# Dense attention scores: the products with the keys' low parts as two tiles of 64 rows, on a copied query

## The chip, the cores and the metric

The kernel runs on one core of a Trainium2 chip. The metric is the device time of one execution in microseconds (us). The kernel before was timed in three runs: 2363.53, 2365.14 and 2366.84 us, a median of 2365.14. One further execution was taken with the hardware profiler; every duration below is from it. Engines in the rows: PE is the tensor engine (PEld its loading of weights), DVE the vector engine, ACT the scalar engine, POOL the GpSimd engine, SP the engine that issues most transfers; an ending q (ACTq, SPq) is an engine's issuing of transfers.

## The reference

A trunk of two layers over 1024 tokens of width 1024. Each layer has three groups of attention heads beside each other (A: four heads with a two-dimensional neighbourhood, B: six with a sliding window, C: six dense heads on two key and value heads), an output projection and a gated feed-forward part. The change is in group C:

```python
q = apply_axial_rope(rms_norm(q, gq), cos, sin)      # (1, 1024, 6 heads, 64)
k = apply_axial_rope(rms_norm(k, gk), cos, sin)      # (1, 1024, 2 groups, 64)
# for each block of 128 queries, R = 3 heads per group
s = jnp.einsum('bqgrd,bkgd->bgrqk', qblk, k).astype(jnp.float32) * scale
p = jax.nn.softmax(s, axis=-1).astype(v.dtype)
return jnp.einsum('bgrqk,bkgd->bqgrd', p, v)
```

So a head has 8 blocks of 128 queries, and each block needs scores against all 1024 keys, a softmax over them, and the product with the values. The computation is in float32.

## The kernel before, in words

**High and low parts.** PE takes the type fp32r here, which holds fewer bits than float32. To keep precision the kernel splits numbers into a high part, rounded to fp32r, and a low part, the remainder. For group C, the tile `qkC[g]` (128 rows, 5 slots, 1024 tokens; one per key group) holds in slots 0 to 2 the three query heads, transposed: rows 0 to 63 are the 64 dimensions of the high part, rows 64 to 127 those of the low part. Slot 3 holds the keys' high part twice, one below the other, and slot 4 the keys' low part twice. One product over all 128 rows with slot 3 so gives (query high + query low) x key high, and one with slot 4 gives (query high + query low) x key low.

**A block of scores.** `c_dots` (line 1356) takes head and block, and makes a tile `sC` of 128 queries by 1024 keys in PSUM: for each half of 512 keys a product with slot 3 and then one with slot 4, which adds to it. These are four products of 128x512 with the same 128x128 weights, the query block. DVE takes the row maximum (`c_max`, a TENSOR_REDUCE into `rs`), ACT the exponential with the row sum (`c_exp`, an ACTIVATE into `pr`), and POOL divides by the sum (`scale_rows`). Then PE transposes the block in eight pieces of 128x128 (tiles `T`, four pieces each), ACT casts each tile of four to its high part (`pt`), DVE subtracts for the low part (also `pt`), and PE multiplies with the values (`pv<-pt,vs`). PSUM has two buffers for `sC`, three for `T` and one for `pv`.

**The order.** Two blocks of a head make a pair (class `PairC`, line 1586); 24 pairs of C come first in a stream, then 16 of A and 24 of B. A loop over n (line 1879) handles pair n: it turns (transposes) pair n, multiplies pair n-1 with the values, and scores the pair three ahead (`AHEAD`). Pairs 0 and 1 are scored earlier, during the projections; pairs 2 and 3 in `opened`, at n = 0. In this stage, from n = 0 to 22, PE, ACT and DVE aren't pinned to the written order: a scheduler orders their instructions ahead of time, by its own estimates. POOL keeps the written order, and so does SP up to n = 6.

**Transfers in that stage.** At n = 0 eight transfers on SP store the values to DRAM (`v_store`, rows `vAd<-vs`); at n = 6 eight bring them back in another layout, for groups A and B (`v_back`, rows `vs<-vAd`). In layer 0, at n = 4, SP also stores a skewed bias table for A and rows for B (`skA<-skr`, `skB<-rowB`). Behind these stand the loads for the first A heads (`qk<-qkd`, `zA<-zAd`). All of SP's and ACT's transfers share eight semaphores (DMAHW0 to DMAHW7), given out in turn; a transfer waits until the transfer before it on the same semaphore has landed. Which of them this is shows from the built program.

The recording helper at line 49 issues every operation, so rows of the profile nearly all have line 49; they are told apart by the tiles' names.

Of the kernel before, what the change touches and what calls it, by code (L numbers as in the profile page):

```python
# [11 lines left out]
F32R = mybir.dt.float32r  # L12
# [7 lines left out]
P = 128  # L20
# [56 lines left out]
def f32(ap):  # L77
    return ap.bitcast(F32)
# [7 lines left out]
def trunk(ctx: ExitStack, tc, A, C, out):  # L86
    nc = tc.nc
    pe, act, dve, pool, sp = (
        Engine(tc, e) for e in (nc.tensor, nc.scalar, nc.vector, nc.gpsimd, nc.sync)
    )  # L90

    def pin(engines, on):
        for e in engines:
            e.pinned = on

    def open_pool(name, bufs=1, side="left", space=None):
        kw = dict(name=name, bufs=bufs, side=side, reuse_waits="tile")
        if space is not None:
            kw["space"] = space
            if space == PSUM:  # L100
                kw.pop("side")
        cm = tc.tile_pool(**kw)
        p = cm.__enter__()
        return cm, p
# [156 lines left out]
    class Ahead:  # L261


        def __init__(self, gen):
            self.gen, self.have = gen, []
# [141 lines left out]
    def rstd_cols(ssqs, width, nt, sp_, psp, tag="mm", newton=False):  # L407

        ps = psp.tile([P, 512], F32, name="ps_st", tag=tag)
        for j in range(nt):  # L410
            for i, s in enumerate(ssqs):
                pe.matmul(
                    ps[:, j : j + 1],
                    s[:, j * P : (j + 1) * P],
                    ones,
                    start=(i == 0),
                    stop=(i == len(ssqs) - 1),
                )
        r = sp_.tile([P, 8], F32, name="rstd", tag="rstd", bufs=2)
        if newton:  # L420
            inv_sqrt(r[:, :nt], ps[:, :nt], width, sp_)
            return r
        act.activation(r[:, :nt], ps[:, :nt], AF.Sqrt, bias=epst, scale=1.0 / width)
        dve.reciprocal(r[:, :nt], r[:, :nt])
        return r
# [592 lines left out]
    for l in range(2):  # L1018
# [14 lines left out]
        def qk_tile():  # L1033
            return qkp.tile([P, 5, S], F32R, name="qk", tag="qk", bufs=2)

        qkC = [qk_tile() for _ in range(2)]
# [313 lines left out]
        def c_scores(h, j, c, pr, rs):  # L1350

            s = c_dots(h, j)
            c_max(s, c, rs)
            c_exp(s, c, pr, rs)

        def c_dots(h, j):

            g = qkC[h // 3]
            s = psS.tile([P, 1024], F32, name="sC", tag="S")
            for kb in range(2):  # L1360
                ks = slice(kb * 512, (kb + 1) * 512)
                for i in range(2):
                    pe.matmul(
                        s[:, ks], g[:, h % 3, j * P : (j + 1) * P], g[:, 3 + i, ks],
                        start=(i == 0), stop=(i == 1),
                    )
            return s

        def c_max(s, c, rs):
            dve.tensor_reduce(out=rs[:, c : c + 1], in_=s, axis=AX.X, op=ALU.max, negate=True)  # L1370
# [61 lines left out]
        for oc in range(NE, 8):  # L1432
            w = wab
            for half in range(2):
# [16 lines left out]
                i = 2 * (oc - NE) + half  # L1451
# [20 lines left out]
        at_cm, atp = open_pool("att", side="right")  # L1472
# [114 lines left out]
        class PairC(Pair):  # L1587
            def __init__(self, h, p):
                super().__init__(10 + h, 6 + h // 3, p)
                self.h = h  # L1590
                self.pr = first_pairs.pop(0) if first_pairs else [None, None]

            def dots(self, c):
                self.s = getattr(self, "s", []) + [c_dots(self.h, 2 * self.p + c)]

            def max(self, c):
                c_max(self.s[c], c, self.rs)
# [152 lines left out]
        class PairA(Band):  # L1750


            name, by_columns = "sA", True
# [11 lines left out]
        class PairB(Band):  # L1765
            name = "sB"
# [109 lines left out]
        AHEAD, AHEAD_B, NC = 3, 4, 24  # L1876
        pin((pool,), True)
        made, done = 0, len(first_pairs)
        scored, worked = [], []
        for n in range(-AHEAD - 1, N + 3):  # L1880
            ahead = AHEAD if n + AHEAD < NC else AHEAD_B
# [25 lines left out]
            else:  # L1907
# [18 lines left out]
                        pairs[n - 1].pv(i)  # L1926
                scored, worked = fresh, scored
            done = max(done, min(begin.stop, made)) if n >= 0 else done
            while made < min(N, n + ahead + 2):
                for key, make in preload.get(made, []):  # L1930
                    heads[key] = make()
                pairs[made] = stream[made][0]()
                made += 1
# [31 lines left out]
            for end, (chunks, width) in norms.items():  # L1965
                if begins[end] <= m <= end and (m - begins[end]) % 8 == 7 and (n <= NC or m >= NC):
                    i = (m - begins[end]) // 8
# [55 lines left out]
        for ki in range(5):  # L2023
# [8 lines left out]
            if ki == 2:  # L2032
                r = rstd_cols([gss[N - 1]], norms[N - 1][1], 8, atp, psl, newton=True)
# [503 lines left out]
        for u in range(NU):  # L2537
            i, t = divmod(u, NB)
# [14 lines left out]
            for j in range(4):  # L2553
                js = slice(j * P, (j + 1) * P)
# [39 lines left out]
        if last_layer:  # L2594
            blocks_ = [(1, j, nh) for j in range(4) for nh in range(2)]
            turned = [out_turn(*b) for b in blocks_[:7]]
            r = rstd_cols(odd, D, 4, ntp, psl)
# [105 lines left out]
```

## Time and profile before

| what | value |
|---|---|
| runs | 2363.53, 2365.14, 2366.84 us; median 2365.14 |
| span of the profiled execution | 2365.0 us |
| PE busy in it | 2324.0 us, 98% |
| DVE, ACT, POOL busy | 1758.8, 1185.8, 778.4 us |
| score products of C (`sC<-qk`) | 384 of 400 ns mean, 106.2 us |
| row maxima of C (`rs<-sC`) | 88 of 1220 ns, 107.4 us |

The span is within the spread of the runs, so the profiled execution can stand for them. A row of a group reads: line, engine, operation, output<-input by the names of tiles, shape, count | busy us, mean ns of one | idle time of the engine just before them, and what ended most of it. A row of the timeline reads: start, duration, engine, line, operation, tiles, count of operations run together, and in brackets the idle time before. PE's operations are pipelined: the recorded length of one is longer than the pace at which they follow each other, so the number of 384 times 400 ns is not time that PE spends on them alone (106.2 us counts overlaps once).

### The profile page before, as it was taken

Reading aid. Unit: us, or ns where it says so; the run is one execution under the profiler, and the core shown is the slowest. Engines: PE = TensorE matmul, PEld = TensorE weight load, DVE = VectorE, ACT = ScalarE, POOL = GpSimd, SP = SyncE. Lnnn points to the kernel's source line nnn. Section 1 sums busy time; section 2 is a strip of 40 time slices with the busy share of each in tenths; the row PEclk is TensorE's granted clock in tenths of the full one; section 3 lists DMA queues with packets and bytes.
Section 4 is the critical chain, followed back from the end, with each engine's and each line's share of the span. In section 5 each row is a group of like instructions: output and inputs, shape, how many; then the busy total and the mean of one; then the engine's idle time right before and its main releaser. Section 6 shows DMA issues by size and latency. Waiting matters only on the chain. (4 is left out here: it accounts for less than half of the span.)

```text
span 2365.0 us, 33492 instructions
## 1 busy us (share of the span) xinstructions
PE 2324.0 (98%) x11804; PEld 1959.2 (83%) x11804; DVE 1758.8 (74%) x2762; ACT 1185.8 (50%) x2262; POOL 778.4 (33%) x749
## 2 busy tenths in 40 slices
PE   9999999999999999999999999999999999999998
PEld 7888898888788888788888889988878888888886
DVE  7878998869867677595767689897796674538765
ACT  5423889845543333344633268896453434334443
POOL 1530447600444445100145134584005444430001
PEclk9999999999999999999999999999999999999999
DMA  8677416162435544775435851333634443339643
GB/s 281 182 213 232 116 34 185 51 210 94 146 121 166 165 138 141 232 233 181 148 102 139 249 177 28 92 104 104 208 98 139 151 147 103 99 107 305 203 120 112
DMA packets 307450, 358.02 MB, mean 151 GB/s; under 512 B 52029, under 2 KB 223901, under 8 KB 307281
## 3 DMA queue, kind: packets, MB, share of 16 engines
q1 hardware_dynamic: 290784, 346.26, 47.1%
q10 hardware_dynamic: 16128, 9.44, 1.5%
q8 instruction: 93, 1.52, 0.3%
q14 instruction: 77, 0.62, 0.1%
q0 software_dynamic: 368, 0.17, 0.0%
HBM read 270.84 MB, written 88.63 MB: 152 GB/s over the span
## 5 line engine op out<-in xcount | busy, mean ns | idle before, releaser
L49 PE MATMUL ps_d<-wpt 128*128 128x512 f32 x1848 | 423.7, 390 | 1.0 <-ACT wpt L49 0.7
L49 PEld LDWEIGHTS ps_d<-wpt 128*128 128x128 f32 x1848 | 345.7, 188 | 74.3 <-issue 3.0
L49 POOL TENSOR_SCALAR pr<-pr,rs 128x1024 f32<-128x1024 f32 (+2 forms) x248 | 190.7, 785 | 186.8 <-DVE rs L49 166.7
L49 POOL TENSOR_TENSOR sg<-sg,u 128x512 f32<-128x512 f32 x82 | 117.2, 1431 | 348.1 <-ACT sg L49 221.6
L49 ACT CAST wpt<-w 128x512 fp32r<-128x512 f32 x154 | 95.7, 621 | 194.5 <-PE ps_d L49 176.1
L49 PE MATMUL pv<-pt,vs 128*128 128x256 f32 x1088 | 174.0, 296 | 14.3 <-DVE y L49 13.0
L49 DVE TENSOR_TENSOR pt<-T,pt 128x512 fp32r<-128x512 f32 x272 | 177.4, 679 | 7.1 <-ACT pt L49 5.9
L49 ACT CAST pt<-T 128x512 fp32r<-128x512 f32 x272 | 151.7, 586 | 42.9 <-PE T L49 41.4
L49 DVE SCALAR_TENSOR_TENSOR acc<-wmt,condT,acc 128x512 f32<-128x512 f32 (+1 forms) x98 | 115.5, 1186 | 77.1 <-DMA wmt<-in_w_mod_dram 76.3
L49 POOL TENSOR_TENSOR wpt<-ws,wpt 128x512 fp32r<-128x512 f32 x80 | 112.8, 1410 | 181.6 <-ACT wpt L49 136.3
L49 ACT COPY u<-ps_w 128x512 f32<-128x512 f32 x128 | 75.1, 587 | 192.6 <-PE ps_w L49 192.6
L49 DVE TENSOR_TENSOR wpt<-w,wpt 128x512 fp32r<-128x512 f32 x154 | 109.0, 708 | 83.8 <-ACT wpt L49 83.8
L49 PEld LDWEIGHTS pv<-pt,vs 128*128 128x128 f32 x1088 | 141.0, 189 | 26.9 <-DVE y L49 24.9
L49 PE MATMUL T<-identr,pr 128*128 128x128 f32 x1176 | 160.1, 273 | 0.8 <-DVE pt L49 0.4
L49 PEld LDWEIGHTS T<-identr,pr 128*128 128x128 f32 x1176 | 137.8, 140 | 15.8 <-issue 1.3
L49 ACT CAST wpt<-ws 128x512 fp32r<-128x512 f32 x176 | 107.7, 622 | 53.3 <-PE ps_w L49 23.4
L49 DVE TENSOR_TENSOR wpt<-graw,wpt 128x512 fp32r<-128x512 f32 x154 | 110.2, 716 | 17.0 <-ACT wpt L49 17.0
L49 DVE TENSOR_TENSOR wpt<-ws,wpt 128x512 fp32r<-128x512 f32 x96 | 85.2, 896 | 47.6 <-ACT wpt L49 47.4
L49 DVE TENSOR_REDUCE rs<-sC 128x1 f32<-128x1024 f32 x88 | 107.4, 1220 | 12.3 <-PE sC L49 10.9
L49 DVE TENSOR_TENSOR ws<-wr 128x512 f32<-128x512 f32 x88 | 80.3, 913 | 48.5 <-POOL wpt L49 45.1
L49 ACT CAST wpt<-graw 128x512 fp32r<-128x512 f32 x154 | 95.0, 617 | 35.2 <-DMA graw<-gpd 31.0
L49 PE MATMUL ps_w<-h22h,wpt 128*128 128x512 f32 x352 | 108.9, 391 | 2.9 <-ACT u L49 1.9
(310 smaller groups left out, 5936.4 us busy)
## 6 DMA issues: line engine op xcount, KB each, us to landing
wr<-in_w_gu_dram SPq DMA_DIRECT2D x92, 512.0 KB, 4.2
gpd<-sg SPq DMA_DIRECT2D x154, 256.0 KB, 4.4
graw<-gpd SPq DMA_DIRECT2D x76, 512.0 KB, 3.8
w<-in_w_down_dram SPq DMA_DIRECT2D x110, 256.0 KB, 5.2
wmt<-in_w_mod_dram SPq DMA_DIRECT2D x48, 512.0 KB, 5.7
qk<-qkd SPq DMA_DIRECT2D x44, 512.0 KB, 7.3
wst<-in_w_o_dram SPq DMA_DIRECT2D x32, 512.0 KB, 4.3
wmt<-in_w_mod_dram SPq DMA_DIRECT2D x64, 256.0 KB, 4.0
```

What stands on the lines that cost most here:

```text
L49: ins = op(*args, **kwargs)
```

## The change

```diff
-        def c_dots(h, j):
-
-            g = qkC[h // 3]
+        def high_again(h, j):
+
+            q = atp.tile([P, P], F32R, name="qd", tag="qd", bufs=10)
+            act.dma_start(
+                f32(q[64:128, :]), f32(qkC[h // 3][0:64, h % 3, j * P : (j + 1) * P])
+            )
+            return q
+
+        def c_dots(h, j, qd=None):
+
+            g, js = qkC[h // 3], slice(j * P, (j + 1) * P)
             s = psS.tile([P, 1024], F32, name="sC", tag="S")
-            for kb in range(2):
-                ks = slice(kb * 512, (kb + 1) * 512)
-                for i in range(2):
-                    pe.matmul(
-                        s[:, ks], g[:, h % 3, j * P : (j + 1) * P], g[:, 3 + i, ks],
-                        start=(i == 0), stop=(i == 1),
-                    )
+            halves = [slice(kb * 512, (kb + 1) * 512) for kb in range(2)]
+            q = g[:, h % 3, js]
+            for ks in halves:
+                pe.matmul(s[:, ks], q, g[:, 3, ks], start=True, stop=False)
+            for kb, ks in enumerate(halves):
+                r = slice(kb * 64, kb * 64 + 64) if qd is not None else slice(0, P)
+                qr = qd[r] if kb and qd is not None else q[r]
+                pe.matmul(s[:, ks], qr, g[r, 4, ks], start=False, stop=True)
             return s
...
                 self.pr = first_pairs.pop(0) if first_pairs else [None, None]
+                self.qd = again.pop((h, p), [None, None])
 
             def dots(self, c):
-                self.s = getattr(self, "s", []) + [c_dots(self.h, 2 * self.p + c)]
+                self.s = getattr(self, "s", []) + [c_dots(self.h, 2 * self.p + c, self.qd[c])]
...
         made, done = 0, len(first_pairs)
+        again, qmade = {}, 6
...
             done = max(done, min(begin.stop, made)) if n >= 0 else done
+            while 0 <= n and qmade < min(NC, n + AHEAD + 4):
+                h, p = divmod(qmade, 4)
+                again[h, p] = [high_again(h, 2 * p + c) for c in range(2)]
+                qmade += 1
             while made < min(N, n + ahead + 2):
```

`c_dots` now issues both products with slot 3 first, over all 128 rows as before, and then both with slot 4. Where a block has a copy `qd`, the slot-4 product for keys 0 to 511 runs on rows 0 to 63 alone (the query's high part with the keys' low part), and the one for keys 512 to 1023 on rows 64 to 127. For that the query's high part has to stand in rows 64 to 127 as well: `high_again` copies it there from rows 0 to 63 of `qkC`, by a transfer within the chip's memory that ACT issues (64 rows of 512 bytes). The product of the query's low part with the keys' low part is left out in these blocks. Each of the two products uses half of the array's rows, at different rows. Pairs 0 to 5 have no copy and keep four products over 128 rows. From pair 6 on, a copy for each of the two blocks is made in iteration n for pair n + 6; it is read when pair n + 6 is scored, three iterations later. There are ten buffers for copies. That makes 36 copies in each layer, 72 in all, on as many blocks.

The first place is PE in the middle of the dense stage, the same in both layers. Before:

```order
L49 MATMUL pv<-pt,vs 128x256 x8
L49 MATMUL sC<-qk 128x512 x4
L49 MATMUL T<-identr,pr 128x128 x8
L49 MATMUL pv<-pt,vs 128x256 x8
L49 MATMUL sC<-qk 128x512 x4
```

and now, at the same place:

```order
L49 MATMUL pv<-pt,vs 128x256 x8
L49 MATMUL sC<-qk 128x512 x3
L49 MATMUL sC<-qk,qd 128x512
L49 MATMUL T<-identr,pr 128x128 x8
L49 MATMUL pv<-pt,vs 128x256 x8
L49 MATMUL sC<-qk 128x512 x3
L49 MATMUL sC<-qk,qd 128x512
```

The round of transposes, value products and scores stays; of the four score products the third is the one on rows 0 to 63, and the fourth takes its weights from the copy.

The second place is ACT where the loop of layer 1 opens (numbers after the names tell buffers apart). Before:

```order
L49 COPY cmb_13078<-pv_13001 64x512 [waits PE_49]
L49 ACTIVATE pr_13081,rs_12948<-sC_13065,rs_12948 128x1024 [waits DVE_49]
L49 CAST pt_13110<-T_13114 128x4x128 [waits PE_49,Activation_49]
L49 CAST pt_13112<-T_13121 128x4x128 [waits PE_49,Activation_49]
L49 ACTIVATE pr_13099,rs_13084<-sC_13093,rs_13084 128x1024 [waits DVE_49]
L49 CAST pt_13110<-T_13142 128x4x128 [waits PE_49]
L49 ACTIVATE pr_13107,rs_13084<-sC_13101,rs_13084 128x1024 [waits DVE_49]
L49 CAST pt_13112<-T_13149 128x4x128 [waits PE_49]
L49 ACTIVATE pr_13140,rs_13109<-sC_13134,rs_13109 128x1024 [waits DVE_49,Pool_49]
```

and now:

```order
L49 COPY cmb_13150<-pv_13073 64x512 [waits PE_49]
L49 ACTIVATE pr_13153,rs_13020<-sC_13137,rs_13020 128x1024 [waits DVE_49]
L49 DMA qd_13156<-qk_11596 64x128 [waits DMAHW7_49]
L49 DMA qd_13158<-qk_11596 64x128 [waits DMAHW1_49]
L49 ACTIVATE pr_13175,rs_13160<-sC_13169,rs_13160 128x1024 [waits DVE_49]
L49 DMA qd_13185<-qk_11596 64x128 [waits DMAHW4_49]
L49 ACTIVATE pr_13183,rs_13160<-sC_13177,rs_13160 128x1024 [waits DVE_49]
L49 DMA qd_13187<-qk_11596 64x128 [waits DMAHW7_49]
L49 CAST pt_13190<-T_13194 128x4x128 [waits Activation_49]
```

Four copies and two exponentials now stand ahead of the first cast. The semaphores that the first three copies wait for belong to the sixth and the eighth store of the values and to the first transfer of the values back.

The third place is SP in layer 0, where the bias rows of B are stored and the values come back. Before:

```order
L49 DMA skA1_92<-skr_90 512x1x512 [waits DMAHW5_49]
L49 DMA skB_95<-rowB_94 128x512 [waits DMAHW6_49]
L49 DMA skB_95<-rowB_94 128x512 [waits DMAHW7_49]
L49 DMA skB_95<-rowB_94 128x512 [waits DMAHW0_49]
L49 DMA skB_95<-rowB_94 128x512 [waits DMAHW1_49]
L49 DMA skB_95<-rowB_94 128x512 [waits DMAHW2_49]
L49 DMA skB_95<-rowB_94 128x512 [waits DMAHW3_49]
L49 DMA vs_1402<-vAd_93 128x1x512 [waits DMAHW4_49]
```

and now:

```order
L49 DMA skA1_92<-skr_90 512x1x512 [waits DMAHW5_49]
L49 DMA skB_95<-rowB_94 128x512 [waits DMAHW2_49]
L49 DMA skB_95<-rowB_94 128x512 [waits DMAHW3_49]
L49 DMA skB_95<-rowB_94 128x512 [waits DMAHW4_49]
L49 DMA skB_95<-rowB_94 128x512 [waits DMAHW5_49]
L49 DMA skB_95<-rowB_94 128x512 [waits DMAHW6_49]
L49 DMA skB_95<-rowB_94 128x512 [waits DMAHW7_49]
L49 DMA vs_1402<-vAd_93 128x1x512 [waits DMAHW1_49,DMAHW0_49]
```

SP's own order is the same. But all 36 copies of the layer have taken their turn on the semaphores ahead of `skB`: the six stores now wait for copies 29 to 34 of the layer, and the first two transfers back for copies 35 and 36.

## Prediction

> **What bounds the kernel now.** I began with the busy times and slices of the page, to see which engine is short of time.
>
> ```profile
> PE 2324.0 (98%) x11804; PEld 1959.2 (83%) x11804; DVE 1758.8 (74%) x2762; ACT 1185.8 (50%) x2262; POOL 778.4 (33%) x749
> PEclk9999999999999999999999999999999999999999
> ```
>
> The tensor engine (PE) is busy 98% of the span, at an undisturbed clock. That is an average over stages, though, and the change touches one, the dense heads, once in each layer. The view by windows, on a steady stretch of it in each layer (columns: PE, weight loads, DVE, ACT, POOL, then clock, DMA share, GB/s), says what is second there.
>
> ```profile
> 250.00:340.00 90.00, 89.90 (x644) 81.38 (x643) 84.02 (x122) 75.52 (x138) 43.57 (x40) 1.00 0.17 46
> 1410.00:1490.00 80.00, 79.90 (x569) 72.17 (x569) 74.17 (x108) 66.76 (x121) 35.49 (x32) 1.00 0.09 22
> ```
>
> PE is full, but DVE is at 93% and ACT at 83%. A faster PE soon meets DVE. The groups of the second stretch turn this into a step:
>
> ```profile
> L49 DVE TENSOR_TENSOR pt<-T,pt 128x512 fp32r<-128x512 f32 x58 | 37.0, 680 | 0.1
> L49 DVE TENSOR_REDUCE rs<-sC 128x1 f32<-128x1024 f32 x29 | 35.4, 1221 | 5.1 <-PE sC L49 4.6
> L49 ACT ACTIVATE pr<-sC,rs 128x1024 f32<-128x1024 f32 x29 | 32.8, 1130 | 1.7 <-DVE rs L49 1.7
> L49 ACT CAST pt<-T 128x512 fp32r<-128x512 f32 x56 | 30.7, 588 | 11.1 <-PE T L49 10.9
> ```
>
> 29 blocks of 128 queries in 80 us make 2.76 us a block. DVE has 74.17/29 = 2.56 us of work in it and idles 0.20, nearly all of it ahead of the row maximum, waiting for PE's scores (sC). ACT has 66.76/29 = 2.30 and idles 0.46, mostly for PE's transposes (T). So PE sets the pace, and at most 0.20 us a block is to be had before DVE does.
>
> PE's own row of work in a block, from the timeline (start, duration):
>
> ```profile
> 1430.58 1.03 PE L49 MATMUL T<-identr,pr 128*128 128x128 f32 x8
> 1431.37 1.20 PE L49 MATMUL pv<-pt,vs 128*128 128x256 f32 x8
> 1432.41 1.09 PE L49 MATMUL sC<-qk 128*128 128x512 f32 x4
> 1433.34 1.03 PE L49 MATMUL T<-identr,pr 128*128 128x128 f32 x8
> ```
>
> From start to start the eight transposes hold PE for 0.79 us, the eight products with the values for 1.04 and the four score products for 0.93: together 2.76, with no gap.
>
> **The change part by part: the score products.** Of four 128x512 products a block, two become 64-row ones that can lie side by side in the array. What one of them costs in a stream is its pace, not its recorded length:
>
> ```profile
> 210.70 1.98 PE L49 MATMUL sC<-qk 128*128 128x512 f32 x8
> 212.51 0.39 PE L49 MATMUL ps_ab<-hh,whi 128*128 128x512 f32 x1
> ```
>
> Eight of them hold PE from 210.70 to 212.51, so 0.226 us each. If the two small ones run fully side by side, a block saves 0.226; if one after the other, nothing. No run of before has two small products on different rows. The only products with fewer rows are two on the same 32, and they follow each other:
>
> ```profile
> 93.33 0.62 PE L49 MATMUL ps_b<-oneh,t5h 32*6 32x512 f32 x2 [0.23 <-DVE qko L49]
> 94.17 0.50 PE L49 MATMUL ps_c<-whi,hh 128*128 128x512 f32 x1 [0.22 <-DVE cq L49]
> 94.50 0.40 PE L49 MATMUL ps_c<-whi,hl 128*128 128x512 f32 x1
> ```
>
> A product with a quarter of the rows takes as long as a full one (0.62 for two, so 0.39 and then 0.23). So half the rows save nothing; only lying side by side does. I take full overlap, because nothing that the two use is common: their weights, their moving rows and their halves of the result are all different.
>
> **Going into and out of the small form.** Each block now goes from 128 rows to 64 and back. The cost is bounded below by 0: PE already goes from score products to transposes to products with values in each block, and 0.93 us for four score products against 4 x 0.226 = 0.90 leaves 0.03 for the change of kind. It is bounded above by a stop and a restart. A stop lets the last product run out: its recorded 0.39 less the pace, 0.17. A restart shows in the row at 94.17: 0.50 against 0.40 for the next, 0.10 for a weight load that nothing covers. That is 0.27 a change, 0.54 a block, more than twice the gain. I take 0.05 a change, nearer the lower row, since in a block nothing waits on a semaphore between the forms and the instructions stand ready. So PE has 2.76 - 0.23 + 0.10 = 2.63 us a block, still above DVE's 2.56; the bounds are -0.20 (where DVE stops it) and +0.54 - 0.23 = +0.31.
>
> The Trainium skill speaks against the change here: "TensorEngine Tiling (Array Packing)", Key Properties, says that a change of the tiling mode, though not of the tile, drains the engine. It names no time, and no trace of before has a change under load; with the run-out of 0.17 twice a block and no bare load the block would come to +0.11. For the overlap, "TensorE: Matmul & The Clock Gate", Part 3, gives 3.07 times for four row tiles; by it two tiles would save about seven tenths of my 0.226 (2 - 2/1.53), an estimate from that page.
>
> Blocks concerned: pairs 6 to 23 of 24 in both layers, 18 x 2 x 2 = 72. **Term 1: 72 x -0.13 = -9.4 us**, bounds -14 and +22.
>
> **Order of the products.** All blocks now have both high products ahead of both low ones. The count of products and of weight loads is the same: 0. The row maximum reads both halves after the last product either way.
>
> **The copies.** 72 transfers of 64 rows of 512 bytes are new, issued by ACT. What ACT pays for one shows where it issues stores of its own:
>
> ```profile
> 218.04 1.12 ACT L49 ACTIVATE pr<-sC,vecs 128x1024 f32<-128x1024 f32 x1
> 218.10 1.24 ACTq L49 DMA_DIRECT2D qkd<-qko  x2
> 219.47 0.60 ACT L49 ACTIVATE qko<-ps_ab 128x512 fp32r<-128x512 f32 x1 [0.22 <-issue]
> ```
>
> An issue takes 0.62 us of the sequencer and runs under the operation ahead of it: two of them began 0.06 after an exponential of 1.12 did and left ACT idle for 0.22. In the new order a copy stands behind an exponential or a cast, mostly alone. So 0 to 0.1 a block is bare, out of 0.46 idle: I take 0. If no cover held, ACT would have 2.30 + 0.62 = 2.92, above the 2.76 of now: +0.16 a block, +12 us, the other bound. The data is wanted three pairs later, about 6 x 2.76 = 16 us, against 2.7 to 6.0 us in the list of DMA issues below. The DMA share is 9% in that stretch, so the transfer itself costs 0.
>
> **The waits that the copies bring.** The eight DMA semaphores go round over all hardware queues; a transfer waits until the one before it on its semaphore has landed. ACT's new copies now fall between SP's stores and loads, and a wait at a copy holds what is queued behind it on ACT.
>
> ```profile
> 1387.27 6.24 SPq L49 DMA_DIRECT2D vAd<-vs  x8
> 1397.17 5.27 SPq L49 DMA_DIRECT2D vs<-vAd  x8
> vAd<-vs SPq DMA_DIRECT2D x16, 256.0 KB, 3.3
> vs<-vAd SPq DMA_DIRECT2D x16, 256.0 KB, 6.0
> qkd<-qko SPq DMA_DIRECT2D x40, 128.0 KB, 2.7
> 1396.71 1.11 ACT L49 ACTIVATE pr<-sC,rs 128x1024 f32<-128x1024 f32 x1
> 1398.76 1.14 ACT L49 ACTIVATE pr<-sC,rs 128x1024 f32<-128x1024 f32 x1
> ```
>
> In layer 1 the first two copies wait for the sixth and the eighth store of the values (vAd), which have landed by about 1397, under the exponential at 1396.71. The third waits for the first transfer of the values back (vs<-vAd): issued at 1397.17, 6.0 us to land, so 1403.2. ACT reaches it after one more exponential, at about 1399, and stands until 1403: 4.2 us. Behind it are the next exponential and the casts of the transposes; PE waits for these, after it has used up the free buffers (a score block of 0.93 and three transpose tiles of four, 3 x 0.40 = 1.2). PE loses 2.1 to 4.2: I take 3. Two later copies wait for the last two of those eight, which land within a microsecond of ACT's arrival: inside the same estimate. In layer 0 the first copies wait for stores that went out from 229.12 on, the eighth for a skew issued behind them:
>
> ```profile
> 229.12 6.29 SPq L49 DMA_DIRECT2D vAd<-vs  x8
> 235.46 0.68 SPq L49 DMA_DIRECT2D skA<-skr  x1
> 243.94 10.87 SPq L49 DMA_DIRECT2D vs<-vAd  x8
> 278.03 1.90 SPq L49 DMA_DIRECT2D qk<-qkd  x3
> qk<-qkd SPq DMA_DIRECT2D x44, 512.0 KB, 7.3
> 357.05 1.45 PE L49 MATMUL sA<-qk 128*128 128x256 f32 x8
> ```
>
> The last store goes out by 235.4 and lands 3.3 later, when the loop begins, so 0 to 2 for late landings; I take 0.5. There it is SP that waits: its six stores of shifted bias rows wait for copies near the end of the stage (about 300 us on), and the values back for the last ones, at about 320. Queued behind are the loads of the first neighbourhood head, before at 278.03. Eight issues back take 5.3 to 10.9 us, so the loads go out by 331 and land by 340; first used at 357.05. The margin of 17 us costs 0; it would cost only what passes 357. **Term 2: +3.5 us**, bounds +0.5 and +6.
>
> **Sum:** 2365.0 (the span) - 9.4 + 3.5 = 2359.1; the median shown, 2365.14, is as good as that span, so 2359.
>
> **The rivals.** (B) The two small products do not overlap, and the change does not do what it says. The row at 93.33 speaks for it as far as it goes (it shows two on the same rows); against it stands that here the rows differ. PE then has 2.76 to 2.86 a block: 0 to +7, with the waits 2365 + 3.5 = 2368 to 2376.
>
> (C) Changing the form stops the array each time, and two stops cost more than the overlap gives. (That is the rule on drains of the Trainium skill's "TensorEngine Tiling (Array Packing)", Key Properties.) For it: a run-out of 0.17 is in every recorded length, and no row shows small weights being set under a full product. Against it: the change of kind at 0.03 already in each block. It decides from 0.113 a change on, half of 0.226. With 0.17 to 0.27 a change the block is +0.11 to +0.31, or +8 to +22, with the waits 2377 to 2391. DVE then idles more, not less.
>
> (D) ACT becomes the bound. For it: 83% busy, and 0.62 more a block has to find cover; copies that wait for PE's last use of a buffer hold ACT too. Against it: the overlap at 218.10 and 0.46 idle. It decides once 0.46 of the 0.62 is bare and PE is no slower than now. It gives at most 2365 + 12 + 3.5 = 2380, and about 2367 where half is bare and eats the gain.
>
> **How the numbers follow.** Forecast (A) 0.52, B 0.16, C 0.22, D 0.10. Within 0.2% is 2360.4 to 2369.9, about what a measurement of this kernel can tell from no change. A's own range is 2352 to 2366 (-14 + 0.5 to -5 + 6); its middle lies near that edge: 0.36 faster, 0.16 same. B: 0.08 same, 0.08 slower. C: 0.22 slower. D: 0.02 same, 0.08 slower. So 0.36, 0.26, 0.38. The range takes A from its lower end and reaches into C to all but its dearest end: 2352 to 2389.
>
> **What would show it.** The four score products from start to start: 0.80 by A, 0.93 to 1.03 by B, 1.04 to 1.24 by C. Two small products starting within some hundredths of each other show the overlap. Step time in the steady stretch: 2.63 by A, with DVE's idle time ahead of the row maximum down to 0.07 a block; 2.87 and more by C. ACT idle for its own issues, and PE waiting for casts, would show D. A hole on ACT from about 1399 to 1403, with PE waiting for casts or exponentials behind it, shows term 2. I am wrong on the margin of layer 0 if the first neighbourhood scores wait for a transfer.

## The result, and the profile after

The change made the kernel slower: a median of 2380.38 us (2379.89 to 2383.06, four runs) against 2365.66 for the kernel before, a ratio of 1.0063 with a 95% interval of 1.0051 to 1.0075. That is +14.7 us, where -6 was forecast. The profiled execution has a span of 2378.1 us, 13.1 more than before.

The page of the kernel after, parts 1 and 2, shows that PE has not become less busy and that its clock is not the cause:

```profile
PE 2332.9 (98%) x11804; PEld 1940.1 (82%) x11804; DVE 1760.1 (74%) x2762; ACT 1187.0 (50%) x2262; POOL 777.4 (33%) x749
PEclk9999999999999999999999999999999999999999
```

Where the time went is read from two marks on PE that both kernels have in each layer: the end of the projections (the last start of `ps_ab<-hh,whi`) and the first sum for the norm of the dense heads' output (the first start of `ps_st<-onesr,gss`), which stands behind the whole stage. The view by tile gives first and last starts. Before, layer 0 and then layer 1:

```profile
L49 PE MATMUL ps_ab<-hh,whi x30: 389/389/393, 200.2 to 225.5; 128*128 128x512 f32 x30
L49 PE MATMUL ps_st<-onesr,gss x32: 169/250/250, 375.5 to 420.8; 128*128 128x1 f32 x32
L49 PE MATMUL ps_ab<-hh,whi x128: 388/389/496, 1227.7 to 1383.8; 128*128 128x512 f32 x128
L49 PE MATMUL ps_st<-onesr,gss x32: 169/250/250, 1532.6 to 1577.8; 128*128 128x1 f32 x32
```

and after:

```profile
L49 PE MATMUL ps_ab<-hh,whi x30: 389/389/393, 200.0 to 225.2; 128*128 128x512 f32 x30
L49 PE MATMUL ps_st<-onesr,gss x32: 169/250/250, 382.9 to 428.2; 128*128 128x1 f32 x32
L49 PE MATMUL ps_ab<-hh,whi x128: 388/389/496, 1235.0 to 1391.3; 128*128 128x512 f32 x128
L49 PE MATMUL ps_st<-onesr,gss x32: 169/250/250, 1546.4 to 1591.7; 128*128 128x1 f32 x32
```

From mark to mark layer 0 took 150.0 us and takes 157.7 (+7.7); layer 1 took 148.8 and takes 155.1 (+6.3). Between the stages nothing changes (225.2 against 225.5 ahead of them, 1008.4 against 1008.3 us between them). So the whole loss lies in the two dense stages: 14.0 us, of which the rest of the span gives back 0.9, most of it behind layer 1.

**The small form.** PE's timeline of a block in the steady part, after (start, duration), and its weight loads:

```profile
1441.87 1.06 PE L49 MATMUL sC<-qk 128*128 128x512 f32 x3
1442.43 0.50 PE L49 MATMUL sC<-qk,qd 64*128 64x512 f32 x1
1442.86 1.10 PE L49 MATMUL T<-identr,pr 128*128 128x128 f32 x8
1443.71 1.19 PE L49 MATMUL pv<-pt,vs 128*128 128x256 f32 x8
1444.74 1.06 PE L49 MATMUL sC<-qk 128*128 128x512 f32 x3
```

```profile
1441.76 0.30 PEld L49 LDWEIGHTS sC<-qk 128*128 128x128 f32 x2
1442.43 0.18 PEld L49 LDWEIGHTS sC<-qk 64*128 64x128 f32 x1 [0.36 <-issue]
1442.43 0.18 PEld L49 LDWEIGHTS sC<-qk,qd 64*128 64x128 f32 x1
1442.86 0.86 PEld L49 LDWEIGHTS T<-identr,pr 128*128 128x128 f32 x8 [0.25 <-issue]
```

The two small products do run side by side: their weights are both loaded at 1442.43, and the pair is done with by 1442.86. But the way in and out eats that. Two full products at 0.226 end their turn at 1442.32; the small form begins at 1442.43, 0.11 later. Its weights are not loaded ahead, as those of the full products are (the loads stood idle for 0.36 and start with the products), so one small product is recorded with 0.50 instead of 0.39, another 0.11. The pair holds PE for 0.43 until the transposes' first weights go in: 0.226 of pace, the 0.11 for the bare loads, and 0.09 on the way back. The eight transposes then take 0.85 instead of 0.79. A step from 1441.87 to 1444.74 is 2.87 us, where it was 2.76.

**The opening.** DVE's timeline where the loop of layer 0 begins, before and after:

```profile
229.25 1.29 DVE L49 TENSOR_TENSOR pt<-T,pt 128x512 fp32r<-128x512 f32 x2 [0.23 <-ACT pt L49]
230.45 1.22 DVE L49 TENSOR_REDUCE rs<-sC 128x1 f32<-128x1024 f32 x1
```

```profile
229.00 1.29 DVE L49 TENSOR_TENSOR pt<-T,pt 128x512 fp32r<-128x512 f32 x2 [0.23 <-ACT pt L49]
232.40 1.23 DVE L49 TENSOR_REDUCE rs<-sC 128x1 f32<-128x1024 f32 x1 [2.11 <-DMA qkd<-qko]
```

The first row maximum of the loop now waits 2.11 us for stores of the projections that have nothing to do with it. The ten buffers for copies were added to the pool that also holds `rs` and `pr`. The reading, which e4 tests below: that pool grew, its tiles moved, and `rs` and `pr` came to lie on memory that the tiles `qko` had held, and that these last stores still read. PE then stands idle for 1.95 us ahead of its next scores. Layer 1 has the same row (2.00 us).

### The profile page after: what moved, and what is told of

Its sections match the earlier page's. It is cut to its first block, busy times and chain, and to the rows that moved or that the text cites. A ratio compares the mean times of both kernels' runs of the same rounds, so it can differ in the third digit from the quotient of the medians.

```text
span 2378.1 us, 33594 instructions
## 1 busy us (share of the span) xinstructions
PE 2332.9 (98%) x11804; PEld 1940.1 (82%) x11804; DVE 1760.1 (74%) x2762; ACT 1187.0 (50%) x2262; POOL 777.4 (33%) x749
## 4 chain that ended last, share of the span: by engine, by line
PE 81%; DVE 9%; issue 4%; ACT 3%; DMA 2%; POOL 1%; SPq 0%; ACTq 0%; POOLq 0%; DVEq 0%
PE ps_w L49 31%; PE ps_d L49 15%; PE ps_o L49 7%; PE ps_ab L49 6%; PE pv L49 5%; PE T L49 4%; PE ps_v L49 4%; PE sC L49 3%; PE ps_c L49 2%; ACT pr L49 1%; DVE y L49 1%; DMA wmt<-in_w_mod_dram 1%; DVE pr L49 1%; DVE pt L49 1%; PE ps_st L49 1%
## 5 line engine op out<-in xcount | busy, mean ns | idle before, releaser
L49 PE MATMUL pv<-pt,vs 128*128 128x256 f32 x1088 | 175.5, 297 | 14.1 <-DVE y L49 13.1
L49 ACT CAST wpt<-w 128x512 fp32r<-128x512 f32 x154 | 95.6, 621 | 173.9 <-PE ps_d L49 158.5
L49 ACT CAST pt<-T 128x512 fp32r<-128x512 f32 x272 | 152.8, 586 | 46.9 <-PE T L49 44.2
L49 PE MATMUL T<-identr,pr 128*128 128x128 f32 x1176 | 165.4, 276 | 2.6 <-DVE pt L49 1.7
L49 PEld LDWEIGHTS T<-identr,pr 128*128 128x128 f32 x1176 | 132.2, 140 | 26.6 <-issue 14.5
L49 DVE TENSOR_REDUCE rs<-sC 128x1 f32<-128x1024 f32 x88 | 107.4, 1220 | 26.6 <-PE sC L49 22.2
L49 DVE TENSOR_TENSOR wpt<-graw,wpt 128x512 fp32r<-128x512 f32 x154 | 110.0, 715 | 16.7 <-ACT wpt L49 16.5
```

Source lines behind the costliest of these rows:

```text
L49: ins = op(*args, **kwargs)
```

## The experiments

Theory F: the loss in the products is the change of form, two changes of about 0.17 us a block against 0.226 from the overlap. Beside it, the copies cost by the waits that they bring. Rival R: the products break even, and the copies cost everything. The table has the length from mark to mark in each layer, from each profiled execution, beside the runs.

| kernel | runs, us | ratio to before (95%) | layer 0 | layer 1 |
|---|---|---|---|---|
| before | | | 150.0 | 148.8 |
| after | 2380.38 | 1.0063 (1.0051 to 1.0075) | 157.7 | 155.1 |
| e1 copies alone | 2378.17 | 1.0050 (1.0035 to 1.0065) | 155.0 | 154.4 |
| e2 small products, no copies | 2370.56 | 1.0018 (1.0009 to 1.0027) | 152.7 | 151.2 |
| e3 both on rows 0 to 63 | 2387.89 | 1.0089 (1.0073 to 1.0106) | 160.8 | 158.7 |
| e4 own pool | 2376.97 | 1.0042 (1.0027 to 1.0057) | 154.5 | 155.4 |
| e5 own pool, POOL issues | 2374.06 | 1.0029 (1.0016 to 1.0043) | 152.7 | 151.8 |
| e10 own pool, SP issues | 2380.88 | 1.0062 (1.0047 to 1.0077) | 164.3 | 151.0 |
| e6 two blocks in one stay, no copies | 2396.27 | 1.0128 (1.0111 to 1.0144) | 164.8 | 163.6 |
| e7 the same with copies, POOL issues | 2399.28 | 1.0139 (1.0124 to 1.0154) | 164.8 | 163.6 |
| e8 as e6, order held | 2385.57 | 1.0083 (1.0067 to 1.0100) | 159.6 | 158.5 |
| e9 as e7, order held | 2387.51 | 1.0088 (1.0073 to 1.0103) | 159.9 | 159.0 |

The kernel before had medians of 2366.12 beside e1 to e4, 2366.35 beside e5 to e7 and 2365.06 beside e8 to e10.

**e1, the copies alone.**

```diff
-                r = slice(kb * 64, kb * 64 + 64) if qd is not None else slice(0, P)
-                qr = qd[r] if kb and qd is not None else q[r]
-                pe.matmul(s[:, ks], qr, g[r, 4, ks], start=False, stop=True)
+                pe.matmul(s[:, ks], q, g[:, 4, ks], start=False, stop=True)
```

> The 72 copies are made as in the change, but nothing reads them: all four score products of a block run over 128 rows. Theory F (form): two changes of the array's form cost 0.34 us a block, the overlap gives back 0.226, so the products are worth +8 of the +15 us and the copies with the waits they bring +6 to +7: this run at 2372 us (2370 to 2374). Theory R (the copies): the products break even and the copies cost it all: 2380. With the products full again, a steady block should take 2.76 us by F, and 2.87 by R.

Measured: 2378.17 us, +12.0, between the two theories and nearer to R; +5.0 in layer 0 and +5.6 in layer 1. So the copies cost about twice what F left for them. A clean block is back at 2.76 us, which is F's sign, but not all are clean. The 10th and the 44th (last) exponential of the loop in layer 0 stand here in ACT's timeline of e1:

```profile
255.66 1.11 ACT L49 ACTIVATE pr<-sC,rs 128x1024 f32<-128x1024 f32 x1 [0.24 <-DVE rs L49]
353.20 1.12 ACT L49 ACTIVATE pr<-sC,rs 128x1024 f32<-128x1024 f32 x1 [0.24 <-DVE rs L49]
```

These 34 blocks take 97.5 us, where they took 95.2 before (the rows stand under e2): 2.87 us each on the mean, R's figure, so that the copies cost 0.07 us a block, 2.3 us in the loop of each layer, beside the opening. A part of it shows as gaps on PE, four in these blocks. Here is one of them, with DVE's row that it waits behind:

```profile
254.34 1.22 DVE L49 TENSOR_REDUCE rs<-sC 128x1 f32<-128x1024 f32 x1 [1.21 <-PE sC L49]
256.31 0.63 PE L49 MATMUL T<-identr,pr 128*128 128x128 f32 x4 [0.53 <-DVE pt L49]
```

PE's transposes wait for a subtraction of DVE, and that stands behind a row maximum that had itself waited 1.21 us for PE's scores. PE's order at this place is another one than in the steady part before, with score products between the transposes of one block. Whether ACT's issues cost this time, or the order that the scheduler makes around them, no run separates.

The costs of e1 and e2 by themselves add up to 16.5 us and the change costs 14.7. In the loop they are not additive: 0.07 us a block each by itself, and 0.11 together (98.8 us for the same 34 blocks of the change).

**e2, the small products alone.**

```diff
-                qr = qd[r] if kb and qd is not None else q[r]
-                pe.matmul(s[:, ks], qr, g[r, 4, ks], start=False, stop=True)
+                pe.matmul(s[:, ks], q[r], g[r, 4, ks], start=False, stop=True)
...
-                again[h, p] = [high_again(h, 2 * p + c) for c in range(2)]
```

> The two products of 64 rows as in the change, but no copy is made: the one on rows 64 to 127 takes the query's low part that stands there as its weights (so the product of the query's high part with the keys' low part is left out for keys 512 to 1023). Theory F: 2365.7 + 72 x 0.115 = 2374 us, with a steady block of 2.87 us. Theory R: within 2 us of the kernel before, 2366, with a block of 2.76.

Measured: 2370.56 us, +4.4: slower, so R is out, but about half of F's +8. PE's timeline of e2:

```profile
1455.91 1.06 PE L49 MATMUL sC<-qk 128*128 128x512 f32 x4
1456.90 1.09 PE L49 MATMUL T<-identr,pr 128*128 128x128 f32 x8
1457.75 1.19 PE L49 MATMUL pv<-pt,vs 128*128 128x256 f32 x8
1458.78 1.06 PE L49 MATMUL sC<-qk 128*128 128x512 f32 x4
```

The steady block is 2.87 us, as in the change. What F had missed is that 2.76 was not the mean of before. The 10th and the 44th (last) exponential of the loop in layer 0, in ACT's timeline, before and then in e2:

```profile
251.53 1.13 ACT L49 ACTIVATE pr<-sC,rs 128x1024 f32<-128x1024 f32 x1
346.75 1.11 ACT L49 ACTIVATE pr<-sC,rs 128x1024 f32<-128x1024 f32 x1 [0.24 <-DVE rs L49]
```

```profile
251.77 1.13 ACT L49 ACTIVATE pr<-sC,rs 128x1024 f32<-128x1024 f32 x1
349.31 1.11 ACT L49 ACTIVATE pr<-sC,rs 128x1024 f32<-128x1024 f32 x1
```

34 blocks took 95.2 us, 2.80 each, and now take 97.5, 2.87 each. So the mean block of before is 0.04 us above its clean one, and that of e2 is not. Of these 1.4 us in 34 blocks the groups of waits show 1.0 before, in each layer, where the weights of the value products wait for DVE (`y`, four times), and none of these in e2: a PE that is slower by more than that doesn't meet such waits any more. So the form costs 0.07 us a block net: 2.7 and 2.4 us in the two layers.

**e3, no overlap.**

```diff
-                r = slice(kb * 64, kb * 64 + 64) if qd is not None else slice(0, P)
+                r = slice(0, 64) if small else slice(0, P)
```

> Both products of 64 rows on rows 0 to 63, no copy. They cannot lie side by side, and the two changes of form stay. Theory F: the overlap of 0.226 us a block is gone, so a block of 2.76 + 0.34 = 3.10 us and 2366 + 72 x 0.34 = 2390 us. Rival: if the two products of the change did not really overlap, this run is as fast as the one with them on different rows, 2374.

Measured: 2387.89 us, +21.8, 17.3 above e2.

```profile
1455.92 1.29 PE L49 MATMUL sC<-qk 128*128 128x512 f32 x4
1457.14 1.09 PE L49 MATMUL T<-identr,pr 128*128 128x128 f32 x8
1457.99 1.20 PE L49 MATMUL pv<-pt,vs 128*128 128x256 f32 x8
1459.03 1.29 PE L49 MATMUL sC<-qk 128*128 128x512 f32 x4
```

A block takes 3.11 us: 0.35 above the 2.76 of before, with as many products one behind the other, so that is the price of going in and out together; and 0.24 above e2's 2.87, so the overlap is worth its whole pace of 0.226. The rival, that the change's small products did not overlap, falls.

**e4, the copies in a pool of their own.**

```diff
+        qd_cm, qdp = open_pool("qd", side="left")
...
-            q = atp.tile([P, P], F32R, name="qd", tag="qd", bufs=10)
+            q = qdp.tile([P, P], F32R, name="qd", tag="qd", bufs=10)
```

> The change, with the buffers of the copies in a pool of their own, so that the row maxima and exponentials stand at the addresses of the kernel before and no longer wait for stores that read the memory under them. Theory: DVE's idle 2.0 and 2.1 us ahead of the first row maximum of the loop is gone in both layers, and about 2 us in each with it: 2376 to 2377 us. Rival: the late opening comes from the order of the instructions or from copies that hold ACT: 2380, with ACT or PE idle by as much at another place of the opening.

Measured: 2376.97 us, 3.4 below the change. DVE's wait at the opening is gone in both layers. In layer 0 that gives 3.2 us (157.7 to 154.5); in layer 1 it gives nothing (155.1 and 155.4), because another wait comes into its place. So the total of 2376 to 2377 came true by luck: about 2 us in each layer was forecast. ACT's timeline in layer 1:

```profile
1403.48 1.12 ACT L49 ACTIVATE pr<-sC,rs 128x1024 f32<-128x1024 f32 x1 [0.65 <-DVE rs L49]
1405.99 0.47 ACTq L49 DMA_DIRECT2D qd<-qk  x1
1406.51 1.11 ACT L49 ACTIVATE pr<-sC,rs 128x1024 f32<-128x1024 f32 x1 [1.83 <-DMA vs<-vAd]
```

The third copy stands at the head of ACT's queue until the first transfer of the values back has landed, and the next exponential behind it starts 1.83 us late; PE's next scores also had to wait for 1.83. This is the hold that the prediction had in its second term. In the change itself it does not appear, since there the exponential ahead of that copy came 2 us later by the wait on the moved addresses: at 1408.23 the exponential and at 1408.24 the copy, with no gap.

**e5, the copies issued by POOL** (own pool as in e4).

```diff
-            act.dma_start(
+            pool.dma_start(
```

> The change with the copies' buffers in a pool of their own and the copies issued by POOL, whose transfers have semaphores of their own: no transfer of SP or ACT waits for a copy or the other way round, and ACT issues none. Known by now: the products in two forms alone cost 2.6 us in layer 0 and 2.8 in layer 1, the own pool alone leaves the change at +11. Theory Q (the rest of what the copies cost is ACT's issues and the waits on the shared semaphores): the 2.3 us in layer 0 and 4.3 in layer 1 beyond the form go, and the run is at 2371 us (2370 to 2373), as the one without copies. Theory X (it is the transfers themselves, in the memory or on the 16 engines): it stays at 2376 to 2378.

Measured: 2374.06 us, above the forecast range. But in the dense stages it does what Q says: 152.7 and 151.8, within 0.6 us of e2 without any copy. The rest is outside of them: from the last start of the last down projection to the end of the span e5 needs 17.9 us (2355.0 to 2372.9), the kernel before 15.6 (2349.4 to 2365.0). PE, DVE, ACT, POOL and SP end as before, so these 2.3 us stand behind the last output's issue; what holds the end there was not followed further. The two other runs with copies issued by POOL, e7 and e9, have 18.0 there, and e6 and e8, the same without copies, 15.5.

**e10, the copies issued by SP** (own pool as in e4).

```diff
-            act.dma_start(
+            sp.dma_start(
```

> The change with the copies in a pool of their own and issued by SP. Theory Q (what remained with the own pool, 2.3 us in layer 0 and 4.3 in layer 1, comes of ACT's queue: its waits on shared semaphores and its issues): gone, so as the run without copies, 2371 us (2370 to 2372), without the 2.3 us at the end that the software queue of POOL had. Rival: the hardware queues or the transfers are what costs, so 2375 or more.

Measured: 2380.88 us, so neither. In layer 1 it is as Q says, 151.0, the same as e2. In layer 0 it takes 164.3, where SP has more to do:

```profile
256.95 5.08 SPq L49 DMA_DIRECT2D vs<-vAd  x8
262.12 29.86 SPq L49 DMA_DIRECT2D qd<-qk  x8
292.04 1.94 SPq L49 DMA_DIRECT2D qk<-qkd  x3
SPq L49 <- PE sC L49: 44.2, 13, 16.8
```

```profile
288.25 2.18 PE L49 MATMUL pv<-pt,vs 128*128 128x256 f32 x16 [1.39 <-DVE y L49]
293.54 1.15 PE L49 MATMUL sC<-qk 128*128 128x512 f32 x3 [2.45 <-ACT pr L49]
297.39 0.69 PE L49 MATMUL T<-identr,pr 128*128 128x128 f32 x2 [1.48 <-POOL pr L49]
```

Eight copies are spread over 30 us of SP's queue, in which they stand among stores and loads, and PE has gaps of 1.4 to 2.5 us from 288 on. The last SP line is from its waits between 255 and 320 us: the queue stood 44.2 us for PE's score products, 16.8 of it at one time. That a copy at its head had to wait until PE was done with one of the ten buffers, and that the work behind it came late, is the reading that fits; the chain of it was not followed to its first link.

**e6 and e7, both blocks of a pair in one stay.** If going in and out costs 0.35 us, four small products in one stay should pay: 0.35 for two blocks against 2 x 0.226.

```diff
+                    both = [c_dots(self.h, 2 * self.p + i, self.qd[i], False) for i in range(2)]
+                    for s, lows in both:
+                        lows()
```

> No copies (weights of the rows 64 to 127 as before the copies: the query's low part, so the product of the query's high part with the keys' low part is left out for keys 512 to 1023), and the four small products of the two blocks of a pair follow each other, so that a pair has two changes of form and not four. Theory F: a pair costs 0.345 for the changes less 2 x 0.226 for the overlap, -0.05 a block, where a block alone was at +0.115: 12 us below the run without copies at most, 2361 to 2364 us, less what DVE (2.56 us of work a block) gives back. Rival: both score tiles are held until the pair's small products are done, so PE runs out of free ones and waits for the exponentials: 2368 or more, with PE idle ahead of sC.

> The same grouping with the right weights: copies in a pool of their own, issued by POOL. Under theory Q and F together within 1 us of the run without copies, 2361 to 2365, the only one of these that beats the kernel before; under X or under the rival of the grouping 2367 to 2374.

Measured: 2396.27 and 2399.28 us, the slowest of all. They say nothing on F: in the order of PE the scheduler had put a small product of the first block ahead of the full ones of the second, so a pair goes into the small form twice and its small products are torn apart.

**e8 and e9, the same with the order held on PE.**

```diff
+                    held, pe.pinned, pe.last = (pe.pinned, pe.last), True, None
                     both = [c_dots(self.h, 2 * self.p + i, self.qd[i], False) for i in range(2)]
...
+                    pe.pinned, pe.last = held
```

> As the run with two blocks in one stay (no copies; the product of the query's high part with the keys' low part is left out for keys 512 to 1023), but the eight score products of a pair keep their order on PE: in the run before, the scheduler had put the small product of the first block ahead of the full ones of the second, so a pair went into the small form twice and its small products did not stand side by side. Theory F (0.345 us for going in and out, 0.226 for each two products side by side): a pair costs 0.345 - 0.452 = -0.107 and 36 of them -3.9: 2362 us if nothing waits. Rival S (the score tiles): both of the two tiles of PSUM are filled together and free together, so PE waits for maxima and exponentials once a pair: 0.3 us a pair or more, 2370 to 2385.

> The same order with the right weights: copies in a pool of their own, issued by POOL. 2.3 us of the single-block version of this came after the last output was issued, the rest of it was within 1 us of the run without copies. So as the run with the order held and no copies, plus 3: 2365 under F, 2373 to 2388 under S.

Measured: 2385.57 and 2387.51 us: rival S. In PE's timeline of e8 a stay costs what F says:

```profile
1444.76 1.29 PE L49 MATMUL sC<-qk 128*128 128x512 f32 x6
1445.98 1.10 PE L49 MATMUL T<-identr,pr 128*128 128x128 f32 x8
```

Two full and four small products hold PE for 1.22 us, two full and two overlapped pairs at 0.226 make 0.90, and 0.32 is left for one stay (with the slower transposes behind it 0.38). So the price belongs to the stay and not to the single small product. But the gain is lost elsewhere, as the groups of waits of e8 from 1420 to 1490 us show:

```profile
PEld sC L49 <- ACT pr L49: 7.3, 16, 1.0
PE sC L49 <- ACT pr L49: 3.6, 8, 0.8
```

Both score tiles are filled and freed together, and PE stands idle for exponentials ahead of its scores, 3.6 us of 70, or 0.3 a pair. A pair of e8 is 0.53 us longer than before in layer 0 (9.6 over 18 pairs), with products that should have saved 0.1, so the idle time is about half of what was lost; the other half is in shorter gaps and later starts that were not added up. No run had more score tiles. No version here beats the kernel before.

## Why the prediction was wrong, step by step

**What bounds the kernel** was right for a clean block: PE sets the pace, and the mean granted clock is 0.998 before and 0.997 after. The work of DVE is not what costs: its idle time ahead of the row maxima grew from 12.3 to 26.6 us.

**The overlap** was right, with 0.226 us forecast and 0.24 measured (e3 against e2).

**Going into and out of the small form** failed, as the step "I take 0.05 a change, nearer the lower row". Measured is 0.35 for two, 0.17 a change on the mean (e3). The bound had been right, the choice in it wrong: a change between score products, transposes and value products, all over 128 rows, was taken as the nearest row, though none of these changes the form. The nearer rows were those of the other bound, a stop and a bare load. By the rows of the block above, the way in costs about 0.22 (0.11 of later start, 0.11 of loads that nothing covers) and the way back about 0.15 (0.09, and 0.06 on the transposes); the change of kind before had cost 0.03 of that. So term 1 was not -9.4. By the steady block it would be 72 x 0.11 = +8, and by e2 it is +4.4, since the kernel before lost 0.04 us a block to waits that a slower PE does not meet. The mean over the stage, 2.80, and not one clean step of 2.76, should have been the base of the sum. Of the 20.6 us between the forecast of -5.9 and the +14.7 measured, 13.8 lie in this term.

This is the rule of the Trainium skill's "TensorEngine Tiling (Array Packing)", Key Properties, that a change of tiling mode drains the engine; the runs agree with it and give it a size, 0.35 us for both ways together. Its other side, that tiles work independently, agrees too.

**Rival C** was what happened on PE, at its cheap end: +0.11 a steady block was the figure priced with 0.17 a change. That the size fits so well is in part luck: it was priced with the run-out of the last product alone and no bare load, where the rows show less than that run-out on the way in (0.11 of 0.17) and bare loads beside it.

**The copies.** That their transfers and SP's late stores cost nothing by themselves was right: e5 has 72 copies and dense stages within 0.6 us of e2's, e7 those of e6 without copies, and in the change the margin in layer 0 held. In SP's timeline of the kernel after

```profile
323.95 8.84 SPq L49 DMA_DIRECT2D vs<-vAd  x8
332.88 1.90 SPq L49 DMA_DIRECT2D qk<-qkd  x3
```

the loads of the first neighbourhood head went out at 332.88, 55 us late and still ahead of their first use at 362.07. That ACT's part in the copies costs nothing was not right. The 10th and the last exponential of the loop in layer 0, in ACT's timelines of e4 and then of e5, where POOL issues:

```profile
253.32 1.11 ACT L49 ACTIVATE pr<-sC,rs 128x1024 f32<-128x1024 f32 x1
352.12 1.12 ACT L49 ACTIVATE pr<-sC,rs 128x1024 f32<-128x1024 f32 x1
```

```profile
252.25 1.13 ACT L49 ACTIVATE pr<-sC,rs 128x1024 f32<-128x1024 f32 x1
349.92 1.11 ACT L49 ACTIVATE pr<-sC,rs 128x1024 f32<-128x1024 f32 x1
```

98.8 against 97.7 us for 34 blocks is 0.03 a block, 1.1 us in each layer; with full products it was 0.07 (e1). Both are inside the bound of 0 to 0.1, where 0 was taken. Whether it is the issues, as in rival D, or the order that the scheduler builds with them, stays open.

**Term 2** failed in size and in place. Forecast were 3.5 us, almost all from ACT held in layer 1. Measured are 12.0 for the copies alone (e1), and 10.3 on top of the small form (14.7 less e2's 4.4). What was not looked for is the pool: ten new buffers moved `rs` and `pr` onto memory that stores still read, 2.1 us of DVE's wait in layer 0 and 2.0 in layer 1. In the trace it is the wait for `qkd<-qko` at the first row maximum of the loop, and it is gone where the copies have a pool of their own (e4). The hold of ACT in layer 1 exists (1.83 us in e4, against 4.2 forecast for ACT), but only where the address wait is not ahead of it. Between e4 and e5 1.8 us in layer 0 and 3.6 in layer 1 went with ACT's part in the copies: 1.1 in each is the loop, 1.83 in layer 1 is the hold; the small rest, in the opening, was not taken apart. Step by step from before to the change, layer 0 loses 2.7 by the form (e2), 1.8 by ACT's part (e5 to e4) and 3.2 by the shared pool (e4 to the change), which makes its 7.7. In layer 1 the steps are 2.4, 3.6 and -0.3, with 0.6 between e2 and e5 that was not assigned, which makes its 6.3; the pool's wait adds nothing there, since the hold of ACT hides behind it.

## What to carry to other kernels

Splitting a product over half the rows pays only if a stay in the small form holds more overlapped work than going in and out costs: here 0.35 us a stay against 0.226 for each two products of 128x512, and gathering two blocks for one stay failed, about half of it on waits for the only two score tiles in PSUM. A new buffer is a change to every tile of its pool: look for new waits at instructions that the edit does not touch. Transfers that share semaphores with another queue bring that queue's waits to the engine that issues them, and when one such wait is removed, the next one in its shadow shows.

## What was not expected of the hardware

Two products of 64 rows on different rows overlap in full even as a single pair of 512 columns (0.24 us gained of a pace of 0.226), yet their weights are not loaded ahead behind products of 128 rows (0.36 us of idle loads each time). And 72 copies issued by POOL left 2.3 us behind the last output that copies issued by ACT or SP did not (tails of 15.0 us after and 15.6 in SP's case, 17.9 to 18.0 in the three runs with POOL).
